# Streaming-encoder layer on one Trainium2 core: root spreads moved inside later groups, first attention operands pipelined, prologue products put behind the first queries and keys

## The chip, the cores and the metric

The program runs on one core of a Trainium2 chip. The metric is device time in microseconds (us), the median of several executions. The engines are TensorE (PE, matrix products; PEld is its weight load), VectorE (DVE), ScalarE (ACT), GpSimd (POOL) and SyncE (SP, which here only issues DMAs). Each runs its own instructions in the order of the program and waits on semaphores for the others.

## The reference

```python
h = rmsnorm(x, norm_mix_g)
proj = h @ w_in                     # u (512), q, k, v (512 each)
y_ssm = s5_mixer(u, ...)            # diagonal complex state space, 32 groups, GELU + sigmoid GLU
y_att = chunked_attention(q, k, v)  # 64-frame chunk + 8 previous, relative bias, softmax
x = x + concat(rmsnorm(y_ssm), rmsnorm(y_att)) @ w_out
x = x + (silu(rmsnorm(x) @ w_gate) * (rmsnorm(x) @ w_up)) @ w_down
out = rmsnorm(x)
```

The sequence has 2048 frames of 1024 channels; all is float32. Each float32 product is made of three faster ones: an operand is split into a rounded part `hi` and a rest `lo` (ACT rounds, DVE subtracts), and `mm3` adds `hi*hi`, `lo*hi` and `hi*lo`.

## The kernel before

Only the first 160 us are touched. There the kernel computes `u`, the input of the state-space part, while it prepares the constants of the scan and the first attention operands.

**u_phase.** The sequence is cut in four blocks b of 512 frames. For each block and each of four row groups f, `group(b, f)` adds 8 x 3 = 24 matmuls of 128x512 into one PSUM bank `ps` (six banks in turn). `operands(b, ..)` makes the block's `hi`/`lo` tiles, q = 0 to 7 (`hi`, `lo` for even blocks, `hi0o`, `lo0o` and so on for odd ones). `squares(b)` sums the squares of the frames on ACT; `sums(b)` takes the inverse root by Newton steps: 14 tiny DVE instructions, from `nv` to the last `no`. `spread_(b)` lays the roots out over the partitions with four PE transposes (`pp<-ident,no`), which ACT copies into `pb` and `rsn`. `evac(b, f)` multiplies a finished bank by `pb` on DVE (`us<-ps,pb`), frees the bank and stores `u` by a POOL DMA. PE, DVE, ACT and the SP queue are pinned to program order here (`k.te`, `k.V`, `k.A`, `k.Q`), so the place where a call is written decides who waits behind whom.

**ssm_prologue** is a generator; `do(n)` takes n steps of it. Its middle part is DVE products of 128x512 or 128x576 (`cm`, `vw`), filled in between the `lo` subtractions. Its last part, run in `att_phase` after the u banks are closed, transposes `vw` on PE (`pp<-ident,vw`, copied by ACT to `bst`) and multiplies `bb` by `vg` (`pp<-vg,bbg`, 64 small matmuls, copied by ACT to `kt`); both go to DRAM for the scan.

**att_phase.** `front[0]` loads and splits the first query and key weights (`w`), `front[1]` runs `hT_unit(0)`: it scales the loaded tile with `rsn` and splits it, eight times, in place of the ring tiles (their names in a row are those of the memory they lie in: `hi0x`, `lo0x`, ..., `xt`). Then `qk_unit(0, 0)` computes the first queries and keys (48 matmuls into `pf`), and its results are laid into `hi0x`, `lo0x`, `hi1x`, `lo1x` (queries) and `hi2x`, `lo2x` (keys), copied to the other half of the partitions by SP DMAs. After that the steps begin: scores (`sc`), exponentials (`s`), transposes (`pt`), products with v, and between them the values (`v_unit(0, 0)`, weights `raw<-in_w_v`, split into `w`, matmuls `pf<-w,hi`) and later units.

The code of before interleaves `first` (the qk unit) with the prologue's last part by

```python
        for n, _ in enumerate(first):
            if n >= PRO:
                next(pro, None)
```

Of the kernel before, what the change touches and what calls it, by code (L numbers as in the profile page):

```python
# [16 lines left out]
P = 128  # L17
# [23 lines left out]
HTA = -12, -9  # L41
HTS = -8, -6
HTP = 2
PRO = 1
LIGHT = 0.8
SL = 1
LPH = 2
# [122 lines left out]
def ssm_prologue(k, ident, S):  # L170
# [3 lines left out]
    with tc.tile_pool(name="pro", bufs=1) as p:  # L174
# [214 lines left out]
            G.tensor_copy(S["sw"][:, n, 1, :], a8[:, 1, :, e])  # L389

        pk = k.pk()
        kt = k.t(pk, "kt", [CH, 8, P], bufs=2)
        nc.gpsimd.memset(kt[:], 0.0)
        for b_ in range(4):
            nc.gpsimd.dma_start(S["kt"][:, 8 * b_ : 8 * b_ + 8, 0], kt[:])
# [8 lines left out]
            nc.sync.dma_start(vgs[b_][:], S["v"].rearrange("q g c n m -> (c n) (q g) m")[:, 8 * b_ : 8 * b_ + 8, :P])  # L404
        yield
        for b_ in range(4):
            yield from transposes(pk, b_, wts[b_])
        for b_ in range(4):
            gs = slice(8 * b_, 8 * b_ + 8)
            vg = vgs[b_]  # L410
            kt = k.t(pk, "kt", [CH, 8, P], bufs=2)
            for g0 in (0, 4):
                ps = k.t(k.pro_psum, "pp", [P, 512])[:].rearrange("p (a b) -> p a b", a=4)
                for g in range(4):
                    k.te.matmul(ps[:CH, g, :], bb[:, 8 * b_ + g0 + g, :], vg[:, g0 + g, :], start=True, stop=True)
                nc.scalar.copy(kt[:, g0 : g0 + 4, :], ps[:CH])
                yield
            V.tensor_tensor(kt[:, :, :CH], kt[:, :, :CH], dm[:, gs], op=ALU.add)
            nc.gpsimd.dma_start(S["kt"][:, gs, 1], kt[:])
        pk.release()  # L420


# [3 lines left out]
def u_phase(k, ident, S, aw, front):  # L426

    tc, nc, io = k.tc, k.nc, k.io
    with ExitStack() as cx:
# [20 lines left out]
                Q.dma_start(xt[:], io["xp"][q * P : (q + 1) * P, 2 * b : 2 * b + 2, :].rearrange("p j c -> p (j c)"))  # L450
            return xts

        def operands(b, xts, work=0):
            X[b] = []
            for q, xt in enumerate(xts):
                hi, lo = pair(b, q)
                A.copy(hi[:], xt[:])
                V.tensor_tensor(lo[:], xt[:], f32(hi[:]), op=ALU.subtract)
                X[b].append((hi, lo))
                do(work)  # L460

        def first(each):
            X[0] = []
# [23 lines left out]
        def mm(b, f, ps, q):  # L487
            fs = slice(f * P, (f + 1) * P)
            mm3(te, ps[:], wh[:, q, fs], wl[:, q, fs], X[b][q][0][:], X[b][q][1][:], q == 0, q == KT - 1)
# [4 lines left out]
        def spread_(b):  # L494
            ps = k.t(psum2, "pp", [P, 512])
            spread(k, te, ps, ST[b], 0)
            pbs[b] = pb = k.t(p1, "pb", [P, 512], bufs=2)
            A.copy(pb[:], ps[:])
            A.copy(rsn[:, 2 * b : 2 * b + 2, :], pb[:].rearrange("p (j c) -> p j c", j=2))

# [2 lines left out]
            V.tensor_tensor(us[:], ps[:].rearrange("p (j c) -> p j c", j=2), pbs[b][:].rearrange("p (j c) -> p j c", j=2), op=ALU.mult)  # L503
            nc.gpsimd.dma_start(S["u"][f * P : (f + 1) * P, 2 * b : 2 * b + 2, :], us[:])

        def group(b, f):
            ps = k.t(psum, "ps", [P, 512])
            for q in range(KT):
                mm(b, f, ps, q)
            return ps  # L510

        pss = [k.t(psum, "ps", [P, 512]) for _ in range(4)]
        pro = ssm_prologue(k, ident, S)

        def do(n):
            for _ in range(n):
                next(pro)
# [3 lines left out]
        operands(1, load(1))  # L521
        squares(0)
        sums(0)
        held = pss
        for b in range(1, 4):
            now = [group(b, 0)]
            spread_(b - 1)
            for f in range(4):
                evac(b - 1, f, held[f])
            if b == 1:  # L530
                with tc.high_priority(offset=-LATER):
                    next(pro)
                xts = load(2)
                squares(1)
                operands(2, xts, 2)
                squares(2)
                sums(1)
            elif b == 2:
                squares(3)
                operands(3, load(3), 1)  # L540
                sums(2)
                sums(3)
                do(8)
            else:
                front[0]()
            now.append(group(b, 1))
            if b == 3:
                spread_(3)
                for f in range(2):
                    evac(3, f, now[f])  # L550
                front[1]()
            now += [group(b, 2), group(b, 3)]
            held = now
        for f in (2, 3):
            evac(3, f, held[f])
        do(48 - 16 - 8 - 8)
    next(pro)
    return pro

# [122 lines left out]
def att_phase(k, ident, S):  # L682
    tc, nc, io = k.tc, k.nc, k.io
    with ExitStack() as cx:
# [20 lines left out]
        def hT_unit(sb, q0=0, q1=KT):  # L705
            hi, lo = hT.setdefault(sb, ([], []))
            ts = slice(sb * SB, (sb + 1) * SB)
            xts = {}
            V, A, Q = (k.V, k.A, k.Q) if sb == 0 else (nc.vector, nc.scalar, nc.sync)

            def load(q):
                if q < q1:
                    x = RING[q] if sb == 0 and q < 2 * DB else None
                    xts[q] = k.t(aw, x, [P, SB]) if x else k.t(aw, "xt", [P, SB], bufs=XB)
                    Q.dma_start(xts[q][:], io["xt"][q * P : (q + 1) * P, ts])

            ahead = 2 if sb else KT
            for q in range(q0, q0 + ahead):
                load(q)
            for q in range(q0, q1):  # L720
                yield
                load(q + ahead)
                xt = xts[q]
                for v, n in zip(hT[sb], ("hi", "lo")):
                    v.append(k.t(aw, f"{n}{q}x" if q < DB and sb % 2 else f"{n}{q}", [P, SB], F32R))
                V.scalar_tensor_tensor(xt[:], xt[:], k.gm[:, q : q + 1], S["rsn"][:, ts], op0=ALU.mult, op1=ALU.mult)
                A.copy(hi[q][:], xt[:])
                V.tensor_tensor(lo[q][:], xt[:], f32(hi[q][:]), op=ALU.subtract)
            yield

        def qk_unit(sb, pr):
            ws = [load_w(sb, n) for n in (pr, 4 + pr)]
            yield
            hi, lo = hT[sb]
            if (sb, pr) == (0, 0):
                ts = [[k.t(aw, f"{n}{q}x", [P, SB], F32R) for n, q in (("hi", hh), ("lo", hh), (("hi", "lo")[hh], 2))] for hh in range(2)]
            else:
                ts = [(k.t(aa, "q2h", [P, SB], F32R, bufs=3), k.t(aa, "q2l", [P, SB], F32R, bufs=3), k.t(aa, "k2", [P, 2 * SB], F32R, bufs=3)) for _ in range(2)]
            qk[sb, pr] = ts
            if sb > 0:  # L740
                for hh in range(2):
                    nc.sync.dma_start(f32(ts[hh][2][:, :SB]), S["k"][(sb - 1) % 2, 2 * pr + hh])
            both = (sb, pr) == (0, 0)
            pss = []
            for c in range(2):
                if c == 0 or not both:
                    cc = range(2) if both else (c,)
                    pss += [k.t(pfs, "pf", [P, 512]) for _ in cc]
                    for q in range(KT):
                        cs = slice(q * P, (q + 1) * P)  # L750
                        for m in cc:
                            wh, wl = ws[m]
                            mm3(k.ta, pss[m][:], wh[:, cs], wl[:, cs], hi[q][:], lo[q][:], q == 0, q == KT - 1)
                            if q == 2 and not both:
                                keep_w(4 * m + pr)
                        if q < KT - 1:
                            yield
                ps = pss[c]
                for hh in range(2):
                    q2h, q2l, k2 = ts[hh]  # L760
                    a = slice(hh * 64, hh * 64 + 64)
                    o = slice(64 - hh * 64, 128 - hh * 64)
                    if c == 0:
                        nc.scalar.activation(q2h[a, :], ps[a, :], AF.Copy, scale=-0.125)
                        nc.vector.scalar_tensor_tensor(q2l[a, :], ps[a, :], -0.125, f32(q2h[a, :]), op0=ALU.mult, op1=ALU.subtract)
                        nc.sync.dma_start(f32(q2h[o, :]), f32(q2h[a, :]))
                        nc.sync.dma_start(f32(q2l[o, :]), f32(q2l[a, :]))
                    else:
                        nc.scalar.copy(k2[a, -SB:], ps[a, :])
                        nc.vector.tensor_tensor(k2[o, -SB:], ps[a, :], f32(k2[a, -SB:]), op=ALU.subtract)  # L770
                        if sb < NSB - 1:
                            nc.sync.dma_start(S["k"][sb % 2, 2 * pr + hh], f32(k2[:, -SB:]))
                if both and c:
                    for n in (0, 4):
                        keep_w(n)
                yield

        QK_N = 1 + 2 * KT
# [136 lines left out]
        pro = u_phase(k, ident, S, aw, (lambda: next(first), operands))  # L915
        pfs = cx.enter_context(tc.tile_pool(name="apf", bufs=2, space=bass.MemoryType.PSUM, reuse_waits="tile"))
        pps = k.pro_psum = tc.alloc_tile_pool(name="apro", bufs=6, space=bass.MemoryType.PSUM, reuse_waits="tile")
        for n, _ in enumerate(first):
            if n >= PRO:
                next(pro, None)  # L920
        v0 = v_unit(0, 0)
        next(v0)
        for _ in pro:
            pass
        pps.release()
# [778 lines left out]
```

## Time and profile before

| | us |
|---|---|
| three runs | 2338.62, 2338.92, 2340.84 |
| median | 2338.92 |
| the profiled execution | 2330.97 |
| its span | 2329.2 |
| mean granted TensorE clock | 0.972 |
| PE busy from 0 to 160 | 128.5 |

The last row adds eight stretches of 20 us (12.11, 18.58, 18.12, 16.07, 20.00, 17.01, 16.67 and 9.94). A timeline row reads: start, duration, engine, line, operation, what is written from what, shape, count; brackets hold how long the engine had been idle before it and what ended that. A matmul row shows about 0.39 us although the next one starts 0.23 us later, since they are pipelined. "SPq" and "POOLq" rows are issues of DMAs.

### The profile page before, as it was taken

The numbers are of one execution on the slowest core, as the hardware profiler recorded it, in microseconds if no ns is written. First come the engines' busy times: TensorE is split into PE (matmuls) and PEld (weight loads), VectorE is DVE, ScalarE is ACT, GpSimd is POOL, SyncE is SP. The second block draws the span as 40 slices with busy tenths as digits, with TensorE's granted clock in tenths as the row PEclk, the third lists the DMA queues.
The fourth block names the chain that finished last, engine by engine and source line by source line (L and its number), as shares of the span: only waits on it lengthen the run. The fifth ranks groups of instructions, "written<-read, shape, count | busy, mean of one in ns | idle before, by whom it ended". The sixth has DMA issues, their size and how long they took to land.

```text
span 2329.2 us, 30456 instructions
## 1 busy us (share of the span) xinstructions
PE 2185.7 (94%) x10568; PEld 1836.0 (79%) x10568; DVE 1480.0 (64%) x2251; ACT 1000.6 (43%) x1675; POOL 1133.1 (49%) x1280
## 2 busy tenths in 40 slices
PE   8978899999997899979999998999999999999996
PEld 6767688898986788768888887788888778888886
DVE  7755555656556756666775668766655365578676
ACT  6335555555557542343333335433333343344332
POOL 3416645455660423565555558555555464445442
PEclk9989999999999999989999999999999989999998
DMA  8877776766653535644454556555433287465552
GB/s 312 260 250 262 218 217 192 221 191 193 192 141 113 170 125 178 227 155 148 163 195 166 186 195 245 194 188 174 148 102 111 90 311 249 163 223 180 204 179 73
DMA packets 214066, 437.00 MB, mean 188 GB/s; under 512 B 27096, under 2 KB 57864, under 8 KB 206808
## 3 DMA queue, kind: packets, MB, share of 16 engines
q1 hardware_dynamic: 209048, 420.89, 54.3%
q0 software_dynamic: 4864, 14.17, 2.0%
q8 instruction: 83, 1.36, 0.2%
q14 instruction: 71, 0.58, 0.1%
HBM read 294.98 MB, written 132.15 MB: 183 GB/s over the span
## 4 chain that ended last, share of the span: by engine, by line
PE 50%; DVE 3%; DMA 2%; issue 1%; POOL 1%; ACT 0%; SPq 0%; DVEq 0%; ACTq 0%; POOLq 0%
PE X L75 19%; PE ps L75 16%; PE Y L75 9%; PE W L75 5%; DVE sa L1553 1%; DMA hd<-hq 1%; DVE lo L167 1%; POOL c L167 0%; DMA lo<-hc 0%; DVE hd L167 0%; DMA hd<-wc 0%; DVE S L1372 0%; DVE acc L1570 0%; DVE g L1437 0%; ACT hd L166 0%
## 5 line engine op out<-in xcount | busy, mean ns | idle before, releaser
L75 PE MATMUL X<-hi,c 128*128 128x512 f32 x1408 | 451.2, 391 | 11.1 <-ACT c L166 6.7
L75 PE MATMUL ps<-hd,hd 128*128 128x512 f32 (+1 forms) x1968 | 435.6, 384 | 7.9 <-DVE hd L167 4.6
L75 PEld LDWEIGHTS ps<-hd,hd 128*128 128x128 f32 x1968 | 361.7, 191 | 80.5 <-DVE hd L167 4.9
L167 POOL TENSOR_TENSOR c<-S,c 128x512 fp32r<-128x512 f32 x176 | 251.0, 1428 | 245.8 <-ACT c L166 243.4
L75 PEld LDWEIGHTS X<-hi,c 128*128 128x128 f32 x1408 | 265.3, 188 | 68.5 <-ACT c L166 7.1
L167 POOL TENSOR_TENSOR hd<-hd 128x1536 fp32r<-128x1536 f32 (+1 forms) x53 | 188.8, 3568 | 210.3 <-ACT hd L166 210.3
L75 PE MATMUL X<-lo,c 128*128 128x512 f32 x704 | 274.9, 391 | 0.0
L167 POOL TENSOR_TENSOR c<-raw,c 128x512 fp32r<-128x512 f32 x132 | 188.0, 1425 | 128.2 <-ACT c L166 105.3
L166 ACT CAST hd<-hd 128x1536 fp32r<-128x1536 f32 (+1 forms) x106 | 147.3, 1392 | 227.3 <-DMA hd<-hq 163.6
L75 PE MATMUL Y<-hi,c 128*128 128x512 f32 x704 | 227.1, 393 | 11.8 <-DVE u L1394 11.8
L1518 DVE TENSOR_TENSOR acc<-acc,ps 128x512 f32<-128x512 f32 x196 | 129.0, 681 | 86.4 <-PE ps L75 84.1
L75 PE MATMUL big<-m,woh 128*128 128x512 f32 x512 | 164.9, 403 | 1.7 <-DVE m L167 1.6
L75 PEld LDWEIGHTS Y<-hi,c 128*128 128x128 f32 x704 | 133.5, 190 | 41.3 <-DVE u L1394 13.5
L75 PE MATMUL pf<-hi,w 128*128 128x512 f32 x416 | 154.5, 422 | 7.2 <-ACT w L166 3.6
L606 POOL TENSOR_TENSOR st<-X,a 128x128 f32<-128x128 f32 (+2 forms) x136 | 47.3, 347 | 228.1 <-ACT X L592 189.8
L166 ACT CAST c<-S 128x512 fp32r<-128x512 f32 x176 | 109.2, 621 | 112.7 <-PE Y L75 59.3
L75 PEld LDWEIGHTS X<-lo,c 128*128 128x128 f32 x704 | 132.8, 189 | 27.6
L1390 ACT COPY u<-X 128x512 f32<-128x512 f32 x132 | 76.9, 584 | 177.3 <-PE X L75 177.3
L844 DVE CUSTOM_DVE_ANT_0 s<-sc,nb 128x640 f32<-128x640 f32 (+4 forms) x128 | 94.5, 738 | 91.0 <-PE sc L75 88.6
L166 ACT CAST c<-raw 128x512 fp32r<-128x512 f32 x132 | 82.1, 622 | 151.1 <-PE Y L75 81.3
L75 PE MATMUL Y<-lo,c 128*128 128x512 f32 x352 | 137.9, 392 | 0.0
L167 DVE TENSOR_TENSOR hd<-hd 128x1536 fp32r<-128x1536 f32 (+1 forms) x53 | 111.8, 2111 | 38.2 <-ACT hd L166 37.9
(463 smaller groups left out, 4684.6 us busy)
## 6 DMA issues: line engine op xcount, KB each, us to landing
w<-wss SPq DMA_DIRECT2D x36, 1024.0 KB, 6.0
hq<-g SPq DMA_DIRECT2D x140, 256.0 KB, 2.1
hd<-hq SPq DMA_DIRECT2D x42, 768.0 KB, 4.5
hd<-wc SPq DMA_DIRECT2D x42, 768.0 KB, 6.0
raw<-in_w_gate SPq DMA_DIRECT2D x44, 512.0 KB, 3.7
raw<-in_w_up SPq DMA_DIRECT2D x44, 512.0 KB, 4.1
wc<-px SPq DMA_DIRECT2D x66, 256.0 KB, 2.9
wss<-w SPq DMA_DIRECT2D x12, 1024.0 KB, 5.7
```

Of the source, the lines that this page charges most:

```text
L75: return self.tc.keep_in_program_order(self.tc.nc.tensor.matmul(*a, **b))
L166: (hi_eng or nc.scalar).copy(hi, raw)
L167: (lo_eng or nc.gpsimd).tensor_tensor(lo, raw, f32(hi), op=ALU.subtract)
L606: eng.tensor_tensor(t[:, :, :, :n], src, ar, op=ALU.mult)
L844: nc.vector.tensor_tensor_reduce(s[:, :nk].rearrange("p (a b) -> p a b", a=nch), ps[:, :nch, :half], hd.nb[:, nk - 1 :: -1].rearrange("p ( ...
L1390: nc.scalar.copy(u[:], ps[:])
L1518: V.tensor_tensor(a, a, ps[:], op=ALU.add)
L1553: (nc.gpsimd if m else nc.vector).tensor_tensor(self.sa[m][:, :n], self.sa[m][:, :n], t[:, :n], op=ALU.add)
```

## The change

It touches the order of work, two buffer counts, and nothing that is computed.

```diff
 def ssm_prologue
-        kt = k.t(pk, "kt", [CH, 8, P], bufs=2)
+        kt = k.t(pk, "kt", [CH, 8, P], bufs=5)
...
         for b_ in range(4):
-            yield from transposes(pk, b_, wts[b_])
-        for b_ in range(4):
             gs = slice(8 * b_, 8 * b_ + 8)
...
             nc.gpsimd.dma_start(S["kt"][:, gs, 1], kt[:])
+        for b_ in range(4):
+            yield from transposes(pk, b_, wts[b_])
 def u_phase
-        def operands(b, xts, work=0):
+        def operands(b, xts, work=0, each=None):
...
                 do(work)
+                if each:
+                    each(q)
...
-            pbs[b] = pb = k.t(p1, "pb", [P, 512], bufs=2)
+            pbs[b] = pb = k.t(p1, "pb", [P, 512], bufs=3)
...
-        def group(b, f):
+        def group(b, f, roots=None):
             ps = k.t(psum, "ps", [P, 512])
             for q in range(KT):
+                if q == 4 and roots is not None:
+                    spread_(roots)
                 mm(b, f, ps, q)
...
-        held = pss
-        for b in range(1, 4):
-            now = [group(b, 0)]
-            spread_(b - 1)
-            for f in range(4):
-                evac(b - 1, f, held[f])
...
+        now = [group(1, 0), group(1, 1, 0)]
+        evacs(0, pss)
+        with tc.high_priority(offset=-LATER):
+            next(pro)
+        xts = load(2)
+        squares(1)
+        operands(2, xts, 2, lambda q: sums(1) if q == 4 else None)
+        squares(2)
+        held = now + [group(1, 2), group(1, 3)]
+        now = [group(2, 0), group(2, 1, 1)]
+        evacs(1, held)
+        squares(3)
+        xts = load(3)
+        do(6)
+        sums(2)
+        sums(3)
+        operands(3, xts, 1)
+        held = now + [group(2, 2), group(2, 3, 2)]
+        front[0]()
+        now = [group(3, 0, 3)]
+        evacs(2, held)
+        front[1]()
+        now += [group(3, f) for f in (1, 2, 3)]
+        evacs(3, now)
+        do(48 - 16 - 6 - 8)
 def att_phase
...
                 A.copy(hi[q][:], xt[:])
-                V.tensor_tensor(lo[q][:], xt[:], f32(hi[q][:]), op=ALU.subtract)
+                if sb == 0 and q:
+                    low(q - 1)
+                if sb or q == KT - 1:
+                    low(q)
...
-                            if q == 2 and not both:
+                            if q == 2:
                                 keep_w(4 * m + pr)
...
-        for n, _ in enumerate(first):
-            if n >= PRO:
-                next(pro, None)
         v0 = v_unit(0, 0)
-        next(v0)
+        for n, _ in enumerate(first):
+            if n == 3:
+                next(v0)
         for _ in pro:
             pass
```

`evacs(b, pss)` calls `evac` for the four groups; `low(q)` is the subtraction that stood there. `keep_w` stores split weights (`wss<-w`) on the SP queue, and `next(v0)` issues the two loads of the value weights; both now stand ahead of the DMAs that duplicate queries and keys.

On PE, in block 1 (`ps_393` is its first bank, `pp` the spread of the roots of block 0). Before:

```order
L75 MATMUL ps_393<-hi7o_362,wul_124 128x512
L78 MATMUL pp_418<-ident_81,no_378 128x128 x4
L75 MATMUL ps_827<-hi0o_334,wuh_123 128x512
L75 MATMUL ps_827<-lo0o_335,wuh_123 128x512
L75 MATMUL ps_827<-hi0o_334,wul_124 128x512
```

Now:

```order
L74 MATMUL ps_393<-hi7o_362,wul_124 128x512
L74 MATMUL ps_418<-hi0o_334,wuh_123 128x512
L74 MATMUL ps_418<-lo0o_335,wuh_123 128x512
...
L74 MATMUL ps_418<-hi3o_346,wul_124 128x512
L77 MATMUL pp_431<-ident_81,no_378 128x128 x4
L74 MATMUL ps_418<-hi4o_350,wuh_123 128x512
```

The spread stood between two groups and now has twelve matmuls of the next group ahead of it; the spreads of blocks 1, 2 and 3 moved in the same way.

On DVE, in `operands(2, ..)` and behind it (`lo_..` are the rests of block 2, `vw` and `cm` prologue products, `nv` to `no` the Newton steps of block 1). Before:

```order
L89 TENSOR_TENSOR lo_262_769<-hi2x_711,hi_261_768 128x512
L89 TENSOR_TENSOR vw_257_762<-cm_259_764,cm_260_765 128x576
L89 TENSOR_TENSOR cm_259_764<-pr_667,ci_141 128x576
L89 TENSOR_TENSOR lo_264_775<-lo2x_712,hi_263_774 128x512
...
L89 TENSOR_TENSOR lo_272_795<-xt_714,hi_271_794 128x512
L89 TENSOR_TENSOR vw_267_788<-cm_269_790,cm_270_791 128x576
L89 TENSOR_TENSOR cm_269_790<-pr_667,ci_141 128x576
L89 TENSOR_SCALAR nv_809<-ss_723 128x4
```

Now:

```order
L88 TENSOR_TENSOR lo_263_794<-hi2x_736,hi_262_793 128x512
L88 TENSOR_TENSOR vw_258_787<-cm_260_789,cm_261_790 128x576
L88 TENSOR_TENSOR cm_260_789<-pr_692,ci_141 128x576
L88 TENSOR_SCALAR nv_799<-ss_748 128x4
...
L88 SCALAR_TENSOR_TENSOR no_802<-nf_800,ny_801 128x4
L88 TENSOR_TENSOR lo_269_818<-lo2x_737,hi_268_817 128x512
L88 TENSOR_TENSOR cm_261_790<-pi_693,cr_140 128x576
```

The Newton steps now stand ahead of the last three rests of block 2 instead of behind them.

On ACT, after the last split of `hT_unit(0)`. Before, twelve `bst` copies stood ahead of the first query copy; from there:

```order
L764 ACTIVATE hi0x_1486<-pf_1492 64x512
L769 CAST hi2x_1488<-pf_1493 64x512
L305 COPY bst_1604<-pp_1605 128x2x2x64
...
L305 COPY bst_1604<-pp_1625 128x2x2x64
L416 COPY kt_1640<-pp_1641 16x512
...
L416 COPY kt_1685<-pp_1692 16x512
L166 CAST w_1629<-raw_1630 128x1024
L166 CAST w_1634<-raw_1635 128x1024
```

Now:

```order
L774 CAST lo2x_1491<-pf_1493 64x512
L413 COPY kt_1568<-pp_1569 16x512
...
L413 COPY kt_1613<-pp_1620 16x512
L304 COPY bst_1628<-pp_1629 128x2x2x64
...
L304 COPY bst_1646<-pp_1659 128x2x2x64
L165 CAST w_1520<-raw_1521 128x1024
L304 COPY bst_1664<-pp_1665 128x2x2x64
...
L165 CAST w_1525<-raw_1526 128x1024
L304 COPY bst_1664<-pp_1677 128x2x2x64
```

The eight `kt` copies come first and all sixteen `bst` copies behind them, with the two casts of the value weights in between.

More of the change, by code (lines that the diff above doesn't have):

```diff
@@ L43 @@
 HTP = 2
-PRO = 1
 LIGHT = 0.8
@@ L406, in ssm_prologue @@
         for b_ in range(4):
-            yield from transposes(pk, b_, wts[b_])
-        for b_ in range(4):
             gs = slice(8 * b_, 8 * b_ + 8)
             vg = vgs[b_]
-            kt = k.t(pk, "kt", [CH, 8, P], bufs=2)
+            kt = k.t(pk, "kt", [CH, 8, P], bufs=5)
             for g0 in (0, 4):
@@ L504, in evac, with evacs @@
             nc.gpsimd.dma_start(S["u"][f * P : (f + 1) * P, 2 * b : 2 * b + 2, :], us[:])
-        def group(b, f):
+        def group(b, f, roots=None):
             ps = k.t(psum, "ps", [P, 512])
             for q in range(KT):
+                if q == 4 and roots is not None:
+                    spread_(roots)
                 mm(b, f, ps, q)
             return ps
+        def evacs(b, pss):
+            for f in range(4):
+                evac(b, f, pss[f])
         pss = [k.t(psum, "ps", [P, 512]) for _ in range(4)]
@@ L523, in u_phase @@
         sums(0)
-        held = pss
-        for b in range(1, 4):
-            now = [group(b, 0)]
-            spread_(b - 1)
-            for f in range(4):
-                evac(b - 1, f, held[f])
[L530 to L556, printed above, removed]
+        now = [group(1, 0), group(1, 1, 0)]
[23 more added lines that the diff above has]
+        do(48 - 16 - 6 - 8)
     next(pro)
@@ L719, in hT_unit, with low @@
                 load(q)
+            def low(q):
+                V.tensor_tensor(lo[q][:], xts[q][:], f32(hi[q][:]), op=ALU.subtract)
             for q in range(q0, q1):
@@ L772, in qk_unit @@
                             nc.sync.dma_start(S["k"][sb % 2, 2 * pr + hh], f32(k2[:, -SB:]))
-                if both and c:
-                    for n in (0, 4):
-                        keep_w(n)
                 yield
@@ L917, in att_phase @@
         pps = k.pro_psum = tc.alloc_tile_pool(name="apro", bufs=6, space=bass.MemoryType.PSUM, reuse_waits="tile")
+        v0 = v_unit(0, 0)
         for n, _ in enumerate(first):
-            if n >= PRO:
-                next(pro, None)
-        v0 = v_unit(0, 0)
-        next(v0)
+            if n == 3:
+                next(v0)
         for _ in pro:
```

## The prediction

> **What bounds the kernel now.** I read the page first, then the waits of PE in the first 175 us (all that the change touches lies there), then the timelines of PE, DVE and ACT, last the DMA issues.
>
> ```profile
> span 2329.2 us, 30456 instructions
> PE 2185.7 (94%) x10568; PEld 1836.0 (79%) x10568; DVE 1480.0 (64%) x2251; ACT 1000.6 (43%) x1675; POOL 1133.1 (49%) x1280
> ```
>
> PE is busy for 94% of the span: the rest of the kernel is PE's, and a shift of its start is handed on to the end. PE's waits from 0 to 175 us (total, times, longest):
>
> ```profile
> PE pp L78 <- DVE us L89: 6.3, 1, 6.3
> PE sc L75 <- ACT kt L416: 4.9, 1, 4.9
> PE pf L75 <- ACT w L166: 4.5, 1, 4.5
> PE pp L78 <- DVE no L89: 3.4, 1, 3.4
> PE pp L78 <- DVE cm L296: 3.3, 1, 3.3
> ```
>
> They are 22.4 us together. The last two are spreads waiting for Newton roots, the first a prologue transpose waiting for a PSUM bank, the other two lie on the way into the steps. The change works on all five. The stretches ahead of the steps (busy of PE, PEld, DVE, ACT, POOL; granted clock, DMA share, GB/s) shows what waiting costs besides: a clock of 0.51. The DMA engines are nearly full there, and two thirds empty 25 us before.
>
> ```profile
> 120.00:130.00 10.00, 6.67 (x23) 5.46 (x24) 9.15 (x16) 2.66 (x8) 4.72 (x8) 0.66 0.35 79
> ...
> 150.00:160.00 10.00, 6.14 (x27) 5.85 (x28) 3.70 (x6) 3.23 (x6) 0.65 (x2) 0.51 0.94 363
> ```
>
> The sum is made against the profiled execution, 2330.97 us (1.8 around its span); the runs' median, 2338.92, is 7.95 above it, and I subtract the same gain from it.
>
> **The change part by part.**
>
> *Spread of block 0.* PE timeline:
>
> ```profile
> 41.88 0.62 PE L78 MATMUL pp<-ident,no 128*128 128x128 f32 x4 [3.29 <-DVE cm L296]
> ...
> 47.92 0.40 PE L75 MATMUL ps<-hi0o,wuh 128*128 128x512 f32 x1
> ...
> 53.50 0.39 PE L75 MATMUL ps<-hi0o,wuh 128*128 128x512 f32 x1
> ...
> 69.00 1.11 PE L78 MATMUL pp<-ident,no 128*128 128x128 f32 x4 [3.42 <-DVE no L89]
> ```
>
> A group of 24 matmuls takes 53.50 - 47.92 = 5.58, one 0.2325. The root comes when it came, so the spread stays at 41.88, but 12 matmuls (2.8) now run in the idle 3.3. Block 2, which began at 53.50 + 5.58 = 59.1, begins at 56.3.
>
> *Spread of block 1.* DVE timeline:
>
> ```profile
> 59.78 0.73 DVE L89 TENSOR_TENSOR lo<-lo2x,hi 128x512 fp32r<-128x512 f32 x1
> ...
> 64.04 0.75 DVE L89 TENSOR_TENSOR lo<-xt,hi 128x512 fp32r<-128x512 f32 x1
> ...
> 66.22 0.26 DVE L89 TENSOR_SCALAR nv<-ss 128x4 f32<-128x4 f32 x1
> ...
> 68.78 0.16 DVE L89 SCALAR_TENSOR_TENSOR no<-nf,ny 128x4 f32<-128x4 f32 x1
> 70.77 2.48 DVE L89 TENSOR_TENSOR us<-ps,pb 128x512 f32<-128x512 f32 x4 [1.82 <-ACT pb L89]
> ```
>
> Newton takes 68.78 + 0.16 - 66.22 = 2.72 and now stands ahead of the row at 59.78. The last three rests of block 2 come 2.7 later; the last, ended at 64.8, ends at 67.5. PE, 2.8 earlier, meets them: group (2, 0) stops at its sixth operand (56.3 + 15 x 0.2325 = 59.8, and the rest is there at 59.78 + 2.72 + 0.73 = 63.2), again at the seventh and eighth, and ends two matmuls after 67.5, at 68.0. The wait for roots has become a wait for operands. Twelve matmuls follow, then the spread: at 70.8 at full clock, where it was at 69.0.
>
> The row at 69.00 shows what such a wait does: four transposes took 1.11 after an idle 3.42, against 0.62 after 3.29. The new stalls are 3.2, 1.4 and 1.5 within 8 us. At the slow pace (1.11 / 0.62 times) the twelve matmuls take 5.0 and the spread comes at 73.0. I take 72.5, nearest to the row at 69.00, whose wait and work the new one resembles most; the bounds are 70.8 and 73.5. From spread to `us` it was 70.77 - 69.00 = 1.8 at the slow clock; with 1.6, `us` of block 1 starts at T = 74.1 (72.1 to 75.3), 3.3 later than before.
>
> The Trainium skill (TensorE: Matmul & The Clock Gate, Part 1, What's actually happening) lets the clock fall after an idle window of some 3.4 us and rise after a busy one, with windows that run free of the program. By this rule no new stall is long enough, T would be 72.1 and the gain 2.0 larger than mine; the rows at 41.88 and 69.00 (3.29 kept the clock, 3.42 lost it) agree with its length, but show nothing of stalls broken by a few matmuls.
>
> *DVE's chain from T to the queries.* These rows carry it:
>
> ```profile
> 76.51 0.69 DVE L89 TENSOR_TENSOR lo0o<-hi0x,hi0o 128x512 fp32r<-128x512 f32 x1 [3.26 <-ACT hi0o L89]
> ...
> 85.42 0.68 DVE L89 TENSOR_TENSOR lo7o<-xt,hi7o 128x512 fp32r<-128x512 f32 x1
> ...
> 99.40 2.35 DVE L89 TENSOR_TENSOR w<-raw,w 128x1024 fp32r<-128x1024 f32 x2
> ...
> 105.68 0.74 DVE L89 SCALAR_TENSOR_TENSOR hi0x<-hi0x,g_mix,rsn 128x512 f32<-128x512 f32 x1
> 107.11 0.69 DVE L89 TENSOR_TENSOR lo<-hi0x,hi 128x512 fp32r<-128x512 f32 x1 [0.69 <-ACT hi L89]
> ...
> 121.99 1.28 DVE L89 TENSOR_TENSOR us<-ps,pb 128x512 f32<-128x512 f32 x2
> 123.19 0.68 DVE L89 TENSOR_TENSOR vw<-cm,cm 128x512 f32<-128x512 f32 x1
> ...
> 133.93 0.69 DVE L89 TENSOR_TENSOR vw<-cm,cm 128x512 f32<-128x512 f32 x1
> ```
>
> A product takes (133.93 - 123.19) / 16 = 0.67. After T: `us` 2.48, six products 4.0, two Newtons 5.4, so block 3's rests start at 86.0 instead of 76.51, one per (85.42 - 76.51) / 7 = 1.27, and the last ends at 95.6. PE's group (3, 0) advances with them to 96.1 and three groups (16.7) follow to 112.8:
>
> ```profile
> 112.03 0.40 PE L75 MATMUL pf<-hi,w 128*128 128x512 f32 x1
> ```
>
> So the u phase itself gains nothing (+0.8); both spreads that are relieved there are paid back by DVE. The gain must come behind it. DVE goes on from 95.6: a product, the weight split 2.35, `us` of block 2 2.48, at 101.1. `hT_unit` took (121.99 - 105.68) / 8 = 2.04 per tile with a gap of 0.69 for ACT's cast; `low(q - 1)` fills the gap, so 1.35 x 8 = 10.8, to 111.9 (121.99 before). The bank of (3, 0) is then freed at 112.5, ahead of PE.
>
> *Queries and keys.* 48 matmuls x 0.2325 = 11.2 without transposes between: 112.8 to 124.0, and the wait of 6.3 is gone, since no transpose stands there. What is late next is DVE: three more `us` (1.9, to 114.4) and 18 rows of products (12.1) to 126.5, then the query and key rests. ACT's second key cast follows the third of these rows (2.1) and takes 0.6, so `kt` copies start at 129.2.
>
> *Prologue tail.* ACT rows, then SP's and the DMA issues (count, KB each, median us to landing):
>
> ```profile
> 132.69 0.65 ACT L305 COPY bst<-pp 128x256 f32<-128x256 f32 x2 [2.14 <-DMA bsts<-bst]
> ...
> 147.38 1.05 ACT L416 COPY kt<-pp 16x512 f32<-16x512 f32 x2 [7.16 <-DMA kts<-kt]
> ...
> 153.34 1.04 ACT L166 CAST w<-raw 128x1024 fp32r<-128x1024 f32 x1 [0.21 <-DMA raw<-in_w_v]
> ```
>
> ```profile
> 86.51 0.78 SPq L89 DMA_DIRECT2D nbms<-nbs  x1
> ...
> 110.83 1.36 SPq L89 DMA_DIRECT2D nbms<-corner  x2
> ```
>
> ```profile
> wss<-w SPq DMA_DIRECT2D x5, 1024.0 KB, 5.9
> ...
> bsts<-bst POOLq DMA_DIRECT2D x4, 512.0 KB, 3.4
> ...
> raw<-in_w_v SPq DMA_DIRECT2D x2, 512.0 KB, 11.7
> ...
> nb<-nbms SPq DMA_DIRECT2D x2, 320.0 KB, 11.0
> ```
>
> With five `kt` buffers the wait of 7.16 goes: eight copies take 4.2, to 133.4. Eight `bst` copies (0.33) end at 136.0, the weight cast 1.04 at 137.0. The ninth `bst` copy reuses a buffer that a DMA empties: stored after the fourth copy (134.7), landed 3.4 later, 138.1, which ends last. Three copies, the second cast and two copies (2.7) free the banks of `sc` at 140.8. PE, with transposes behind the copies, has nothing else to do here: about 11 us after 129 are exposed that used to lie under `pf`.
>
> SP is moved too: the copy of the bias table goes out only after block 3's last rest (96.3 instead of 86.51). It had landed when the corners went at 110.83, so it takes at most 24.3 and lands by 120.6; the last three `vg` loads, queued behind, still land before the seventh `kt` tile (132). The value weights follow them, not the query copies. If they land 11.7 after about 126, the first cast waits until 138, 1.9 more; at the least 0. I take 0, since the `bst` store, at 138.1, hides nearly all of it.
>
> The steps start here:
>
> ```profile
> 148.01 0.47 PE L75 MATMUL sc<-hi2x,hi0x 128*128 128x128 f32 x1 [4.90 <-ACT kt L416]
> ...
> 154.44 0.58 PE L75 MATMUL pf<-w,hi 128*128 128x256 f32 x1 [0.68 <-DVE w L167]
> ...
> 159.52 0.41 PE L75 MATMUL sc<-hi2x,hi0x 128*128 128x256 f32 x1
> ```
>
> Scores at 140.9; value matmuls at 141.2 (154.44 before, 13.2 earlier), with the clock low as before; they take the same 159.52 - 154.44 = 5.1, to 146.3. The second scores wait for the first softmax row on DVE, which now stands behind the first value split (1.2: 147.5) and needs the bias `nb`. SP issues `nb` right behind the second weight store (at 142.2, after the second split). Its bounds are 3.4 and 11.0; behind one store I take 6.5, nearest to the store's 5.9: 148.7, scores at 149.0. **Against 159.52 that is 10.5 earlier**; from there the instructions are those of before, so the end moves alike: 2338.92 - 10.5 = **2328.4**.
>
> **The rivals.**
>
> *Closer packing.* If the clock holds (T = 72.1) and `nb` lands in 3.4, 2.0 + 1.2 come on top (DVE's split then ends last): 2325.2; with bits of the `bst` wait overlapped, 2323. For it: 79 GB/s from 120 to 130, where the stores now go. Against it: 363 GB/s from 150 to 160.
>
> *Late by a part.* T at 75.3 (1.2), value weights 1.9 late, `nb` at 8 (1.5): 4.6 lost, 2333.0.
>
> *Hidden anyway.* The steps' later units are paced by loads and the scan; if those keep their times, the 10.5 are waited out later: 2338.9. Against it: PE's 94%, and those loads are issued by the same queues behind the same work.
>
> *Slower: the DMA crowd.* The same bytes move in some 12 us less, and two landings are now in series on the path: the `bst` store ahead of the ninth copy, and `nb` behind a 1 MB store. Each us more there is a us lost; at 10.5 the gain is gone, at 15.2 the kernel is slower by 0.2%. With 11.7 for the store (8.3 more), 11.0 for `nb` (4.5) and the value weights 1.9 late it is 14.7: 2343.1; a little beyond, 2344. Against it: the store's own row is 3.4, and it goes by POOL's queue, not by SP's.
>
> **How the numbers follow.** Forecast (2325 to 2331) 0.55; closer packing (2323) 0.12; late by a part (2333) 0.16; hidden, or a crowd that takes about all (2339) 0.12; crowd beyond (2344) 0.05. A measurement of this kernel can tell about 0.2%, 4.7 us: faster by more is below 2334.2, the first three cases, 0.83; the same 0.12; slower 0.05. The range runs from 2322.5 to 2337.0: below it lies half of the closer packing, above it the last case and two thirds of the fourth.
>
> **What would show it.** The spreads of blocks 0, 2 and 3 without a wait of over 1 us; in group (2, 0) three stalls on DVE `lo`; block 3's rests starting near 86; `pf` starting near 113, no earlier than before; `hT` tiles at 1.35; no `kt` wait on its DMA; the ninth `bst` copy behind its store; first scores near 141, second near 149. It is wrong if `pf` starts past 116, if `bst` or `nb` take over 10, or if later stretches hand the time back.

## The result and the profile after

| | before | after |
|---|---|---|
| runs, first comparison | 10 | 10 |
| median us (lowest to highest) | 2337.85 (2333.17 to 2340.84) | 2327.52 (2322.68 to 2335.04) |
| ratio, 95% interval | | 0.9963 (0.9950 to 0.9977) |
| ratio, second comparison (12 runs against 35) | | 0.9981 (0.9968 to 0.9995) |
| the profiled execution, its span | 2330.97, 2329.2 | 2327.38, 2325.6 |

The kernel is faster, by 8.7 us by the first ratio and 4.4 by the second; the intervals overlap from 0.9968 to 0.9977, some 5 to 7.5 us. (The ratios are estimated from all runs of a comparison. The two medians of the first one stand further apart, 10.3 us.) PE's waits in the first 175 us of the changed kernel (total, times, longest):

```profile
PE ps L74 <- ACT hi L475: 7.9, 1, 7.9
PE pp L77 <- ACT bst L304: 7.5, 1, 7.5
PE ps L74 <- DVE lo L88: 4.1, 3, 2.8
PE sc L74 <- DVE mn L846: 4.0, 1, 4.0
PE sc L74 <- ACT bst L304: 1.1, 1, 1.1
PE pp L77 <- DVE cm L295: 1.0, 1, 1.0
```

The first line is the start of the program, 7.8 before. The five waits of before that the prediction lists are gone or small, and others stand there: transposes wait for the copies of `bst`, the second scores for the first softmax row (`mn`). PE's, DVE's and ACT's timelines at the places that the prediction names:

```profile
42.33 0.62 PE L77 MATMUL pp<-ident,no 128*128 128x128 f32 x4 [0.97 <-DVE cm L295]
...
63.47 0.51 PE L74 MATMUL ps<-lo,wuh 128*128 128x512 f32 x1 [2.84 <-DVE lo L88]
65.54 0.80 PE L74 MATMUL ps<-lo,wuh 128*128 128x512 f32 x1 [0.92 <-DVE lo L88]
...
112.23 0.40 PE L74 MATMUL pf<-hi,w 128*128 128x512 f32 x1
...
144.10 0.48 PE L74 MATMUL sc<-hi2x,hi0x 128*128 128x128 f32 x1 [1.10 <-ACT bst L304]
...
153.79 0.55 PE L74 MATMUL sc<-hi2x,hi0x 128*128 128x256 f32 x1 [3.98 <-DVE mn L846]
```

```profile
73.66 2.48 DVE L88 TENSOR_TENSOR us<-ps,pb 128x512 f32<-128x512 f32 x4 [4.75 <-ACT pb L88]
...
85.62 0.69 DVE L88 TENSOR_TENSOR lo0o<-hi0x,hi0o 128x512 fp32r<-128x512 f32 x1
...
100.05 0.75 DVE L88 SCALAR_TENSOR_TENSOR hi0x<-hi0x,g_mix,rsn 128x512 f32<-128x512 f32 x1
...
110.47 2.65 DVE L88 TENSOR_TENSOR us<-ps,pb 128x512 f32<-128x512 f32 x4
...
153.35 0.29 DVE L846 CUSTOM_DVE_ANT_0 s<-sc,nb 128x128 f32<-128x128 f32 x1 [2.67 <-POOL XG L634]
```

```profile
127.61 4.17 ACT L413 COPY kt<-pp 16x512 f32<-16x512 f32 x8
131.68 2.21 ACT L304 COPY bst<-pp 128x256 f32<-128x256 f32 x8
135.88 1.04 ACT L165 CAST w<-raw 128x1024 fp32r<-128x1024 f32 x1 [1.99 <-DMA raw<-in_w_v]
141.46 0.92 ACT L304 COPY bst<-pp 128x256 f32<-128x256 f32 x3 [4.54 <-DMA bsts<-bst]
```

T, the rests and `pf` are within 0.6 us of the forecast. Then the ninth `bst` copy comes at 141.46. The DMA issues (median us to landing in the last column) and the timelines of POOL and SP say why:

```profile
bsts<-bst POOLq DMA_DIRECT2D x4, 512.0 KB, 8.0
```

```profile
133.12 0.57 POOL L307 DMA_DIRECT2D bsts<-bst  x1 [0.21 <-ACT bst L304]
...
153.14 0.11 POOL L634 MEMSET XG<- 128x4 f32 x1 [7.44 <-DMA bsts<-bst]
```

```profile
95.28 0.79 SPq L88 DMA_DIRECT2D nbms<-nbs  x1
...
108.94 9.97 SPq L403 DMA_DIRECT2D vg<-vs  x1
119.01 1.36 SPq L88 DMA_DIRECT2D nbms<-corner  x2
120.59 3.01 SPq L403 DMA_DIRECT2D vg<-vs  x3
123.65 2.56 SPq L88 DMA_DIRECT2D wss<-w  x2
126.26 2.18 SPq L693 DMA_DIRECT2D raw<-in_w_v  x2
...
145.02 0.71 SPq L817 DMA_DIRECT2D nb<-nbms  x1
```

In the kernel before, SP's first issue of a `vg` load is short:

```profile
108.73 2.00 SPq L404 DMA_DIRECT2D vg<-vs  x1
```

In the changed kernel this one issue stands for 9.97. The copy of the bias table had gone out at 95.28 (86.51 before), 13.7 ahead of it instead of 22.2. The runs sort by that: where the copy goes out by 87.1 (before, e2, e9, e12), the issue takes 2.0 to 2.2; where it goes out after 94 and the issue follows at 108 to 111, it takes 6.5 to 10.2; in e4 and e11, where the issue comes only at 117 and 118, it takes 2.2 again. So an issue seems to stand while the copy, queued ahead of it, is on its way; what holds it there no row names. SP then comes to the corners, which overwrite parts of the copied table, at 119.01, and 3 MB of weight stores and loads follow from 123.65 on. The loads among them are still on their way when the first `bst` store goes out, at 133.12: the cast at 135.88 had to wait for the first of them. Two stretches of the changed kernel (granted clock, DMA share and GB/s at the end):

```profile
130.00:140.00 10.00, 4.38 (x39) 3.80 (x37) 1.79 (x3) 4.78 (x13) 2.71 (x5) 0.96 1.01 371
140.00:150.00 10.00, 6.83 (x30) 6.22 (x30) 1.23 (x1) 3.49 (x10) 1.06 (x2) 0.53 0.94 360
```

### The profile page after: what moved, and what is told of

It reads as the page before. It is cut to its first block, busy times and chain, and to the rows that moved or that the text cites. A ratio compares the mean times of both kernels' runs of the same rounds, so it can differ in the third digit from the quotient of the medians.

```text
span 2325.6 us, 30451 instructions
## 1 busy us (share of the span) xinstructions
PE 2191.2 (94%) x10568; PEld 1839.8 (79%) x10568; DVE 1481.0 (64%) x2251; ACT 1000.5 (43%) x1675; POOL 1130.8 (49%) x1280
## 4 chain that ended last, share of the span: by engine, by line
PE 50%; DVE 3%; DMA 1%; issue 1%; POOL 1%; ACT 1%; SPq 0%; DVEq 0%; ACTq 0%; POOLq 0%
PE X L74 19%; PE ps L74 16%; PE Y L74 10%; PE W L74 5%; DVE sa L1554 1%; DVE lo L166 1%; DMA hd<-wc 1%; POOL c L166 0%; DMA acc<-x 0%; DVE S L1373 0%; DVE g L1438 0%; DMA hd<-hq 0%; DMA lo<-hc 0%; DVE acc L1571 0%; DVE u L1395 0%
## 5 line engine op out<-in xcount | busy, mean ns | idle before, releaser
L166 POOL TENSOR_TENSOR c<-raw,c 128x512 fp32r<-128x512 f32 x132 | 188.1, 1425 | 128.1 <-ACT c L165 100.6
L74 PEld LDWEIGHTS Y<-hi,c 128*128 128x128 f32 x704 | 133.7, 190 | 40.5 <-DVE u L1395 12.6
L74 PE MATMUL Y<-lo,c 128*128 128x512 f32 x352 | 138.2, 393 | 0.0
```

The source lines that it names most:

```text
L74: return self.tc.keep_in_program_order(self.tc.nc.tensor.matmul(*a, **b))
L166: (lo_eng or nc.gpsimd).tensor_tensor(lo, raw, f32(hi), op=ALU.subtract)
```

## The experiments

All marks are us in the profiled execution of each run: first `pf` matmul, first `kt` copy, first `bst` store and the ninth copy that waits for it, issue of `nb`, first and second scores, first store of `ya` (the first head pair's result).

| run | ratio to before | pf | kt | bst store, 9th copy | nb | scores | ya |
|---|---|---|---|---|---|---|---|
| before | | 112.0 | 138.2 | 128.8, 132.7 | 143.0 | 148.0, 159.5 | 208.9 |
| e9 before again | one run | 112.0 | 138.3 | 129.3, 133.1 | 145.1 | 145.0, 159.8 | 208.8 |
| after | 0.9963 (0.9950 to 0.9977) | 112.2 | 127.6 | 133.1, 141.5 | 145.0 | 144.1, 153.8 | 205.3 |
| e5 after again | 0.9981 (0.9968 to 0.9995) | 114.3 | 129.7 | 135.0, 144.3 | 147.9 | 146.8, 157.1 | 208.3 |
| e1 u phase alone | 0.9998 (0.9986 to 1.0010) | 117.5 | 137.5 | 129.1, 133.0 | 145.0 | 144.4, 159.5 | 209.3 |
| e2 tail alone | 0.9976 (0.9961 to 0.9992) | 111.8 | 131.4 | 137.2, 140.2 | 143.7 | 142.6, 151.9 | 201.6 |
| e3 two kt buffers | 0.9981 (0.9967 to 0.9996) | 111.7 | 127.0 | 139.7, 142.8 | 144.0 | 144.8, 152.7 | 202.1 |
| e4 four bst buffers | 0.9972 (0.9959 to 0.9985) | 111.6 | 127.3 | 133.7, none | 140.2 | 138.7, 149.5 | 200.7 |
| e6 Newton last | 0.9979 (0.9963 to 0.9996) | 112.5 | 127.9 | 133.7, 141.4 | 144.9 | 143.8, 154.2 | 205.3 |
| e7 loads late | 0.9991 (0.9976 to 1.0006) | 111.8 | 127.1 | 132.4, 144.6 | 146.2 | 147.5, 155.3 | 208.0 |
| e8 low undone | 0.9991 (0.9976 to 1.0006) | 116.5 | 132.7 | 138.6, 141.6 | 145.1 | 144.0, 153.3 | 204.0 |
| e10 fewer bytes | 0.9985 (0.9973 to 0.9997) | 112.1 | 127.4 | 136.9, 144.9 | 146.5 | 148.3, 156.4 | 205.9 |
| e11 nb early | 0.9999 (0.9987 to 1.0011) | 112.3 | 128.1 | 134.5, none | 142.4 | 140.4, 150.3 | 200.0 |
| e12 two parts | 0.9981 (0.9971 to 0.9990) | 111.2 | 137.7 | 127.2, 132.1 | 138.9 | 142.5, 149.7 | 201.9 |

**The two halves.** `u_phase` of the changed kernel in the kernel before, and the reverse.

> The u phase of the changed kernel, all behind it as before. Theory (DVE's chain): pf starts where it started, near 112, and block 3's operands for the attention are done some 4 to 5 us sooner than before (100 + 8 x 2.04 = 116.4 against 121.99), so the bank wait of 6.3 on PE shrinks to about 2 and the run ends 4 to 5 us sooner, near 2333. Rival (the front is worth nothing, the tail is all): the kt wait on its DMA takes the place, 2337.9, ratio within 0.999 to 1.001.

Both theories missed where. PE's and ACT's timelines:

```profile
117.49 0.77 PE L75 MATMUL pf<-hi,w 128*128 128x512 f32 x1 [4.84 <-DVE us L89]
```

```profile
152.08 1.04 ACT L166 CAST w<-raw 128x1024 fp32r<-128x1024 f32 x1 [4.37 <-DMA raw<-in_w_v]
```

Without the pipelining `pf` waits for a bank that `us` frees, 5.5 late. The first scores come 3.6 sooner than in the first profile of before, but only 0.6 sooner than in its second (e9, 145.0). The value weights, loaded behind the query copies, come when they came before, and so do the second scores (159.5). The rival has the time, 0.9998.

> The u phase of before, with the pipelined hT unit and the new tail. Theory (DVE's chain): hT starts at 105.7 as before and runs at 1.3 a tile to 116.2, some 5.7 later than in the changed kernel; two us and the products follow, so the kt copies start about 3 later (130.5 for 127.6), and 5 to 6 of the 8.7 us gained are left, near 2331. Rival (the tail is all): 2327.5, as the changed kernel, with the kt copies late under a wait that hides it.

The `kt` copies start late as expected (131.4), yet the second scores come 1.9 before those of the full change. With the old `u_phase` the table copy goes out at 87.11, the `vg` issue is short, the weight stores go out at 115.64, and `bst` stores land in 3.2:

```profile
87.11 0.78 SPq L88 DMA_DIRECT2D nbms<-nbs  x1
...
108.51 2.24 SPq L403 DMA_DIRECT2D vg<-vs  x1
...
115.64 2.21 SPq L88 DMA_DIRECT2D wss<-w  x2
```

```profile
bsts<-bst POOLq DMA_DIRECT2D x4, 512.0 KB, 3.2
```

At the marks the rival holds; the time (5.6 us gained) is the theory's number, and cannot decide, since the ratio cannot be told from the full change's. The u phase's new order gave nothing that could be measured, and its later table copy took from the tail.

**Buffers.**

```diff
-        kt = k.t(pk, "kt", [CH, 8, P], bufs=5)
+        kt = k.t(pk, "kt", [CH, 8, P], bufs=2)
```

> The changed kernel with two kt buffers as before. Theory: the third and the fourth kt tile wait for the store of the first and second; the wait of 7.16 seen before comes back as about 6 ahead of the bst copies, and the run ends 5 to 6 us later, near 2333. Rival (the bst store and the bias table set the end anyway): second scores still near 154, 2328.

The wait is back (6.99 on ACT), and the rival holds: the `bst` store goes out 6.6 later, when the crowd has passed, and lands in 3.1 instead of 8.3, so the second scores do not come later (152.7).

```diff
-            bst = k.t(pk, "bst", [P, 8, 2, NS], bufs=2)
+            bst = k.t(pk, "bst", [P, 8, 2, NS], bufs=4)
```

> The changed kernel with four bst buffers in place of two, so no bst copy waits for a store. Theory (my missed 4.8 us are a chain: late bst store, late last transpose, late issue of nb): the wait of 4.54 goes, transposes end near 137.5 for 142.4, nb goes out near 140 for 145, the second scores come at 149 for 153.8, 2323. Rival (a crowd: the DMA engines are full from 120 to 160 and nb lands when its bytes are served): nb still lands near 152 to 153, second scores near 153, 2327.

The chain is as the theory has it: `nb` at 140.16, the second scores at 149.46. DVE's first softmax row waits for `nb` here:

```profile
149.01 0.29 DVE L846 CUSTOM_DVE_ANT_0 s<-sc,nb 128x128 f32<-128x128 f32 x1 [3.53 <-DMA nb<-nbms]
```

The run (0.9972) lies between the two ratios of the unedited kernel; whether the 4.3 us at this mark reached the end cannot be told.

**The same kernels again.**

> No edit: the changed kernel once more, for a second profile. In its first profile the lead over before is 3.6 at the first store of ya (205.3 against 208.9) and 0.0 at the eighth (464.2 against 464.3), though the runs' ratio is 0.9963. Theory (the clock: slices of 0.74, 0.91 and 0.91 stood there where before had 0.83, 1.00 and 1.00, and such slices fall by chance): the tail repeats, first scores at 144 and second at 153 to 154, but the lead at the eighth store is another one, anywhere from 0 to 8. Rival (later units wait for loads or the scan and hand the lead back): the lead at the eighth store is again within 1 of zero.

> No edit: the kernel before once more, for a second profile of it. The two profiles of the changed kernel have their second scores at 153.8 and 157.1 and the first store of ya at 205.3 and 208.3. Theory (executions of one kernel differ by some 3 us already in the first 210 us, by the clock granted there): before's first store of ya comes 1 to 4 away from 208.9. Rival (before is steady and only the changed kernel, with its crowd of DMAs, scatters): within 1 of 208.9.

Before repeats its mark (208.84, as its rival has it), but is 3.1 later at the eighth store of `ya` (467.37 against 464.27). The changed kernel came 3 later already in the tail, and at the eighth store it was 2.6 behind before's first profile: outside both expectations. Its group (2, 0) stalled longer:

```profile
65.06 0.80 PE L74 MATMUL ps<-lo,wuh 128*128 128x512 f32 x1 [3.86 <-DVE lo L88]
```

The clock granted from 66 to 76 was 0.62 against 0.75, and `us` of block 1 came at 75.76. So one profile of a kernel is good to some 3 us, and a difference of spans (3.6) is no measure of the gain. In the first pair of profiles the 3.6 arise behind the last store of `ya` (754.76 before, 756.35 in the changed kernel), where nothing was changed.

**The Newton steps.** `sums(1)` moved behind `squares(2)`.

> The changed kernel with block 1's Newton steps behind the rests of block 2, as before. Theory (DVE's chain sets the u phase, and the Newton steps ahead of three rests cost it): the rests end at 64.8, group (2, 0) at 65.3, the root comes at 68.9 when twelve more matmuls are done (68.1); us of block 1 starts at 70.8 for 73.7, the first rest of block 3 at 82.8 for 85.6, pf at 109.4 for 112.2, and the first scores 2 to 3 sooner, 2325. Rival (the wait for the root drops the clock as at 69.0 before, and the DMAs behind set the end): us at 72 to 73.5, pf past 111, 2327.5.

DVE's timeline:

```profile
72.59 1.89 DVE L88 TENSOR_TENSOR us<-ps,pb 128x512 f32<-128x512 f32 x3 [2.96 <-ACT pb L88]
75.57 0.69 DVE L88 TENSOR_TENSOR us<-ps,pb 128x512 f32<-128x512 f32 x1 [1.09 <-DMA u<-us]
...
85.89 0.69 DVE L88 TENSOR_TENSOR lo0o<-hi0x,hi0o 128x512 fp32r<-128x512 f32 x1
```

T comes only 1.1 sooner, and the fourth `us` then waits 1.09 for a buffer whose store has not landed; block 3's rests and `pf` stay where they were, as the rival has it. The place of the Newton steps shows no gain here.

**Two orders of the tail.** e7 puts `keep_w` and `next(v0)` back behind the copies; e8 calls `low(q)` right behind its cast.

> The changed kernel with the query and key weight stores and the value weight loads behind the query and key copies, where they stood before. Theory (they are worth their place): the value weights land 4 to 7 later, their casts near 143, value matmuls near 149 for 144.6, the run 3 to 4 later, 2331. Rival (the crowd of DMAs was made by them): the bst store lands in 3.4 for 8.0 and the transposes end 4 sooner; the second scores come no later than 153.8, 2327 or less.

The value matmuls come when the theory has them (149.31; the casts not, at 148.18 for 143), and the second scores 1.5 later: the stores and loads now went out from 129.56 on, around the first `bst` store, whose copy started 12.2 after it. The ratio is not told apart from the full change's.

> The changed kernel without the pipelining of hT: each rest right behind its own cast again, 2.04 a tile for 1.27. Theory (DVE's chain leads to the tail): hT ends 5 to 6 later (116 for 110.5), the kt copies start near 131 for 127.6, the second scores 3 to 4 later, near 157, 2331. Rival (the DMA landings behind set the end and the chain has slack): second scores within 1 of 153.8, 2327.5.

The `kt` copies are 5.1 late, and the second scores 0.5 early: at this mark the rival. The time does not decide: the median, 2333.39, leans to the theory's 2331, but the ratio (0.9991) is not told apart from the full change's. The `bst` store went out at 138.56, 5.4 later than in the changed kernel, and its copy started at the same time:

```profile
141.55 0.92 ACT L304 COPY bst<-pp 128x256 f32<-128x256 f32 x3 [1.28 <-DMA bsts<-bst]
```

**Fewer bytes.** `load_w` does not keep weights 0 and 4 and loads them raw in every block.

> The changed kernel with the first query and key weights not stored (2 MB less written near 124); blocks 1 to 3 load and split the raw weights again instead, six casts and six subtractions more. Theory (bytes waiting in the DMA engines set the landings: at 355 GB/s 2 MB are 5.9 us): the first bst stores land in 3 to 4 for 8.0, the ninth bst copy starts near 137 for 141.5, nb goes out near 141 for 145, the second scores come 3 to 5 sooner, near 150. Rival (POOL's queue or the ring of its stores is slow by itself after the kt stores): landing 7 to 8 and the ninth copy past 140, as now. The whole run: 2325 by the first, less what the six extra splits cost.

Undecided for the theory: with the queue shorter, SP issued the value weights' stores sooner, again ahead of the `bst` store, which took 8.0 to its copy (136.87 to 144.91).

```profile
134.16 2.93 SPq L703 DMA_DIRECT2D wss<-w  x2
```

The rival, a POOL queue that is slow by itself after the `kt` stores, is answered by e2: the same four `kt` stores go out there at 133.01 to 136.42, right ahead of the `bst` store at 137.16, and its copy follows 3.0 later.

**nb ahead of the stores.** Four `bst` buffers, and in `v_unit`:

```diff
-                if i == 0:
+                if i == (2 if sb + fh == 0 else 0):
```

> The changed kernel with four bst buffers, and the two stores of the value weights moved behind two groups of value matmuls, so that nb is queued behind one 0.5 MB load instead of two 1 MB stores. Theory (nb's landing is what the second scores wait for, and bytes ahead of it set it): nb goes out near 139, lands 5 to 6 later, first scores at 138.7, second near 146 for 149.5 with four buffers alone and 153.8 in the changed kernel: 2321. Rival (the value matmuls and the first softmax row take the place): second scores at 149, as with four buffers alone.

The rival has the second scores (150.3), and the run gained nothing. The first store of `ya` comes 8.9 sooner than before, the third only 0.8 (282.69 against 283.50). The order of SP's issues changed far behind the edit: in the changed kernel two `xt` loads go out at 150.39, here none does before 213.02, and two more follow at 248.74. DVE waits for `xt`:

```profile
265.79 1.46 DVE L728 SCALAR_TENSOR_TENSOR xt<-xt,g_mix,rsn 128x512 f32<-128x512 f32 x2 [3.24 <-DMA xt<-in_xt]
```

From 200 to 283 us PE's waits for the `hi` and `lo` tiles made from these loads add up to 8.9, against 5.3 in the changed kernel. That is a part of the loss; the rest stays open.

**Two parts alone.** In the kernel before:

```diff
-        kt = k.t(pk, "kt", [CH, 8, P], bufs=2)
+        kt = k.t(pk, "kt", [CH, 8, P], bufs=5)
...
-                            if q == 2 and not both:
+                            if q == 2:
...
+            if n == 3:
+                next(v0)
```

> The kernel before with two parts of the change alone: five kt buffers, and the weight stores and value weight loads ahead of the query and key copies. The u phase, hT and the order of transposes and kt products stay as before. Theory (these two terms of the tail are the gain): kt copies run without a wait from 138.2 to 142.4, value weights are split by 146, first scores near 143 (148.0 before), second near 150 to 151 (159.5 before), the ratio near 0.997, as the changed kernel's. Rival (the gain needs the transposes behind the queries and keys, since they hold the copies until 138): second scores past 155, ratio 0.999 or more.

The theory holds at every mark, and the ratio equals that of the full change in its second comparison. SP's and PE's timelines:

```profile
86.24 0.79 SPq L89 DMA_DIRECT2D nbms<-nbs  x1
...
114.46 2.75 SPq L89 DMA_DIRECT2D wss<-w  x2
117.25 2.22 SPq L694 DMA_DIRECT2D raw<-in_w_v  x2
```

```profile
142.49 0.33 PE L75 MATMUL sc<-hi2x,hi0x 128*128 128x128 f32 x1
...
149.72 0.28 PE L75 MATMUL sc<-hi2x,hi0x 128*128 128x256 f32 x1
```

The table copy is early, the 3 MB go out nine us sooner, and without any of the other edits the second scores come 4.1 before those of the changed kernel.

## Why the prediction was right, and where its steps were not

The forecast was 2328.4, the median 2327.52. The closeness is in part luck. The forecast gain of 10.5 is near the distance of the two medians (10.3) and inside the first interval, but the ratios say 8.7 and 4.4, and it lies outside the second interval. The ten runs of before have a median 1.07 below the three that the sum started from. And at the mark that the sum is made for, the second scores, the gain was 5.7 in one profile and 2.4 in the other.

- *Spread of block 0*: at 42.33 for 41.88, as forecast.
- *Spread of block 1*: T 74.1 forecast, 73.66 measured; the stalls were 2.84, 0.92 and 0.31 for 3.2, 1.4 and 1.5. The clock fell on them: a matmul row of 0.80 us, and 0.75 granted from 66 to 76. In e6 it fell with stalls of 0.30, 1.32 and 1.17 too (0.76). So the rows decide for the slow pace. The Trainium skill (TensorE: Matmul & The Clock Gate, Part 1, What's actually happening) lets the clock fall after an idle window of about 3.4 us. No stall here was that long; by that rule alone T would have been 72.1.
- *DVE's chain*: rests from 85.6 for 86.0, `hT` 1.30 a tile for 1.35, `pf` 112.2 for 112.8. The start of the rests is right by errors that cancel: T came 0.4 sooner, the six products took 4.5 for 4.0 (they are the longer ones, of 128x576), the two Newtons 5.05 for 5.4. That the u phase itself gains nothing agrees with e1 (0.9998) and e2.
- *Prologue tail*: no `kt` wait, copies from 127.6 for 129.2. **The step that failed** is the landing of the `bst` store: "stored after the fourth copy (134.7), landed 3.4 later". It went out at 133.12 and its copy started 8.3 later. The first scores came at 144.1 for 140.9.
- *nb*: "behind one store I take 6.5". It went out at 145.02 (142.2 forecast) and the first softmax row started at 153.35, 8.3 later; the second scores came at 153.8 for 149.0. The sum also overlooked a wait. The row at 153.35 names the POOL memset of `XG`, which had itself waited for the last `bst` store (7.44), so in this profile that store and `nb` are not told apart. In the second profile (e5), as in e4, the row names `nb`:

```profile
156.70 0.29 DVE L846 CUSTOM_DVE_ANT_0 s<-sc,nb 128x128 f32<-128x128 f32 x1 [3.32 <-DMA nb<-nbms]
```

- *The table copy*: that it goes out later was foreseen, and the corners came at 119 for "by 120.6". Not foreseen was that an issue on SP stands behind it, and what that does to the 3 MB: with the old u phase (e2, e12) they go out from 114 to 116 on, with the new one, where nothing else moves them, from 120 to 126 on, into the stores of the tail. So the crowd, the slower rival, was there in part: 4.9 more for the store and up to 1.8 for `nb`, where it would have needed 10.5. The argument that the `bst` store "goes by POOL's queue, not by SP's" is refuted: the later it goes out behind the last of the 3 MB, the sooner, by and large, its copy follows. In the changed kernel it went out 4.7 us behind, and its copy followed after 8.3 (4.9 and 9.4 in e5); in e12 7.8 behind, and after 4.9; in e2, e3 and e8 eleven or more behind, and after 3.1 at most; in e7, amid the loads, after 12.2. The DMA engines moved 371 GB/s at a share of 1.01 while the store waited. The Trainium skill (DMA: Bandwidth & Descriptors, Issuing engines are not separate DMA queues) says that the DMAs of these queues run on the same DMA engines. The trace agrees, with these 8.3 against 3.0 in e2.
- *From there the end moves alike*: e2 and e12 have the first `ya` store 7 us sooner and ratios of 0.9976 and 0.9981, so more than half of their lead reaches the end; e11 lost its lead. For the changed kernel itself no profile shows it: at the last store of `ya` its two profiles stand at 756.35 and 756.39, those of before at 754.76 and 757.85. That its gain comes from the tail rests on the ratios of e1, e2 and e12, and how much of its lead is kept between 210 and 755 us stays open.

That e2 differs from the changed kernel by `u_phase` alone shows that this order brings the crowd. That the later table copy is what does it is argued from the rows, not shown: a changed kernel with the table copy issued earlier was not run.

## What to carry to other kernels

A median landing time holds for the traffic it was measured in: where a change moves large transfers on a queue, add up the bytes that will be in flight when a waited-for store goes out, whatever engine issues it. Follow a late wait down its queue: here the issue of one 512 KB load stood for 10 us behind the copy of a bias table that `nb` reads only 50 us after it went out, and all later transfers of SP stood with it. Before keeping a large reordering, try its smallest parts; two edits of a few lines gave the gain of the whole, as far as these runs tell (0.9981 for both).

## What the runs showed of the hardware

The granted clock fell on stalls far shorter than 3 us when only a few matmuls stood between them: after 0.30, 1.32 and 1.17 within 6 us in e6 the next 10 us had 0.76. How long a store takes depended on what was on its way when it went out: issued at 133.1 and, in e8, at 138.6, it freed its buffer at 141.5 both times. A DMA's issue on SP took 2.0 to 2.2 us or, behind a 2.5 MB copy that had gone out some 13 us before, 6.5 to 10.2. Executions of one kernel differed by 12 us (2322.68 to 2335.04), and by 3 us at 144 us into the span.
